# RWKV WKV on one core: k and v loads, stores and state rows on other DMA queues

## The chip, the core and the metric

The kernel runs on one NeuronCore of a Trainium2 chip. The metric is the device time of one execution in microseconds (us), as the median of several executions. Engines are named as in the profile: PE (matrix engine), DVE (vector engine), ACT (scalar engine), POOL (GpSimd) and SP (the engine that here only issues transfers). A transfer that POOL issues goes through the software queue q0, one that SP issues through the hardware queue q1; both feed the same 16 DMA engines.

## The reference

A running weighted mean over time, for each of 16 batches and 256 channels, over 2048 time steps:

```python
for b in range(batch):
    aa, bb, pp = 0, 0, -1e38          # per channel
    for t in range(seq_len):
        kk, vv = k[b, t, :], v[b, t, :]
        ww = u + kk
        qq = np.maximum(pp, ww)
        e1, e2 = np.exp(pp - qq), np.exp(ww - qq)
        output[b, t, :] = (e1 * aa + e2 * vv) / (e1 * bb + e2 + 1e-08)
        ww = pp - w + kk
        qq = np.maximum(ww, kk)
        e1, e2 = np.exp(ww - qq), np.exp(kk - qq)
        aa, bb, pp = e1 * aa + e2 * vv, e1 * bb + e2, qq
```

k, v and the output are float32, 16 x 2048 x 256: 33.5 MB each, so some 100 MB go between HBM and SBUF.

## The kernel before

Time lies on the partitions. The 2048 time steps are cut into a head of 32 and 16 steps of 126 (two halves of 63). A step's 16 batches are taken as four *pairs* of four batches each, so one pair is a tile of 126 time rows by 4 x 256 channels; loads take 128 rows where there are 128 left, and 126 in the last step. The head is cut into two special pairs that come third and fourth. `pairs` holds all 66 in the order in which they are worked.

For a pair n, `load(n)` (L108) brings k into `kr` and v into `vr`. `round_k` (L264, the copy on L271) rounds k on DVE, `logs` (L273) forms logarithms of weights as matmuls with constant matrices (PE, L287), `exps` (L294) exponentiates them into the tile `ez` (ACT, L303), `cast_v` (L307) casts v to `vb` on DVE (L311), and `times_v` (L314) multiplies the weights by v on DVE (L319). `sums` (L338) adds up a step's pairs on PE (L349). From these sums a small chain on PE, ACT and DVE (L356 to L461) computes the state that the step hands on. `carries` (L444) forms the state's weights as a tile `ab`, `turn_carries` (L453) turns it on PE, and `inject` (L458) copies it to `row` (L460) and sends it by DMA (L464) into two spare rows, `TC` and `TC + 1`, of the `ez` tiles of the step, so that the output matmuls take it in as if it were two more time rows. A step has two groups of `ez` tiles, j = 0 and 1, of two pairs each, and two rows, h = 0 and 1, for its halves.

Ten iterations after its load stage a pair is finished: `den` (L483, matmuls on L488) and `num` (L503, L509) on PE, `recip` (L492) as a logarithm and an exponential on ACT (L499, L500), `mult` (L513, L517) on DVE, and `store` (L519, L535) writes `rd` to the output.

The main loop (L580 to L621) interleaves all this by hand: iteration n loads pair n + 4, exponentiates pair n, sums pair n - 1, rounds and logs pair n + 1, and finishes pairs n - 10 and n - 11. The function `K` (L35) pins each engine's instructions in the order in which they are written, so every queue is in order, POOL's and SP's too.

What the change touches, by queue:

- SP carries, in order: k and v of the first two pairs, the ten small transfers of the head pairs (L122), k of pair 4, v of all pairs from 4 on, and, once per step, the four transfers of `inject` (L464). The very last store's second half goes on SP too.
- POOL carries the constants at the start, k from pair 5 on, and the stores, and computes nothing else in the steady part.
- `kpool` and `vpool` have four buffers, so the k load of pair n + 4 waits until `round_k(n)` has read its buffer, and the v load until `cast_v(n)` has. `rpool` has five, so `recip` of a pair waits until the store of the fifth pair before it has landed.
- A queue's transfers use eight completion semaphores in turn; a transfer waits until the eighth before it has landed.

Of the kernel before, what the change touches and what calls it, by code (L numbers as in the profile page):

```python
# [9 lines left out]
BF16 = mybir.dt.bfloat16  # L10
# [12 lines left out]
def kernel(  # L23
# [11 lines left out]
    def K(ins):  # L35

        block, e, new = nc.cur_bb.bb, ins.ins.engine, []
        for i in reversed(block.instructions):
            if i.engine == e:
                new.append(i)  # L40
                if i.name == pinned.get(e):
                    break
        for a, b in zip(new[1:], new):
            tc.add_manual_dep(b, a.name, mybir.DependencyInfo(
                mybir.DependencyClass.NoSync, mybir.DependencyReason.DATA), reason="order")
        pinned[e] = new[0].name
        return ins

    PE, DVE, SC, POOL, SP = nc.tensor, nc.vector, nc.scalar, nc.gpsimd, nc.sync
# [3 lines left out]
    TC = 2 * HS  # L53
# [6 lines left out]
    AHEAD = 4  # L60
# [14 lines left out]
    tiny = ctx.enter_context(tc.tile_pool(name="tiny", bufs=1))  # L75
# [18 lines left out]
    NP = len(pairs)  # L94
    kr_of, vr_of = {}, {}

    def is_head(n):
        return pairs[n][0] < 0

    def tiles_of(n):  # L100
        return 1 if pairs[n] == (-1, 1) else 2
# [6 lines left out]
    def load(n):  # L108
        kr = kpool.tile([128, 4, Dm], F32, tag="kr", name="kr")
        vr = vpool.tile([128, 4, Dm], F32, tag="vr", name="vr")  # L110
        kr_of[n], vr_of[n] = kr, vr
        c, p = pairs[n]
        if is_head(n):
            if p == 1:
                K(POOL.memset(kr[64:96, 0:2, :], 0.0))
                K(POOL.memset(vr[64:96, 0:2, :], 0.0))
            for t, x in ((kr, k), (vr, v)):
                for g in range(NG):
                    b = 6 * g + 4 * p
                    e = min(b + 2 * tiles_of(n), B)  # L120
                    if b < e:
                        K(SP.dma_start(out=t[g * GB:(g + 1) * GB, 0:e - b, :],  # L122
                                        in_=x[b:e, 0:T0, :].rearrange("n t d -> t n d")))
        else:
            t0 = T0 + c * TC
            r = min(128, T - t0)
            for t, x, eng in ((kr, k, SP if n <= AHEAD else POOL), (vr, v, SP)):
                K(eng.dma_start(  # L128
                    out=t[0:r, :, :], in_=x[4 * p:4 * p + 4, t0:t0 + r, :].rearrange("n t d -> t n d")))


# [9 lines left out]
    for n in range(2):  # L141
        load(n)
# [3 lines left out]
    def matrix(name, dt, width=128):  # L146
        return consts.tile([128, width], dt, tag=name, name=name)
# [53 lines left out]
    for n in range(2, AHEAD):  # L201
        load(n)
# [38 lines left out]
    Id, IdN, Lh, LhN, Lf, LfN = [matrix(x, BF16) for x in ("Id", "IdN", "Lh", "LhN", "Lf", "LfN")]  # L241
# [20 lines left out]
    EZ, X_of, KM = {}, {}, {}  # L262
# [67 lines left out]
    def group_of(c, j):  # L330
        return 2 * j if c == 0 else 1 + 2 * c + j
# [22 lines left out]
    st, AB = {}, {}  # L354
# [88 lines left out]

    def carries(c):  # L444

        ab = tiny.tile([128, 4, 2, 16], BF16, tag="ab16", name="ab16")
        f, f2 = st.pop((c, "phi")), tiny.tile([128, 2, 32], F32, tag="phi2", name="phi2")
        K(DVE.scalar_tensor_tensor(f2, st[c, "g"][:, 0:2], 1.0, f, ALU.max, ALU.min))
        K(DVE.tensor_mul(ab, AB[c].rearrange("p q h (j x) -> p (h j) q x", j=2),
                         f2.rearrange("p h (j x) -> p (h j) x", j=2).unsqueeze(2).broadcast_to([128, 4, 2, 16])))  # L450
        st[c, "ab"] = ab

    def turn_carries(c):  # L453
        d = bank("num", [128, D]) if wide else bank("den", [128, 2, D])[:, 0]
        K(PE.matmul(d[:, 0:128], st.pop((c, "ab")).rearrange("p m q x -> p (m q x)"), Id, start=True, stop=True))
        st[c, "d"] = d

    def inject(c):  # L458
        row = small.tile([128, 128], BF16, tag="row", name="row")
        K(DVE.tensor_copy(row, st.pop((c, "d"))[:, 0:128]))  # L460
        for j in range(2):  # L461
            for h in range(2):
                p = 64 * h + 32 * j
                K(SP.dma_start(out=EZ[group_of(c, j)][TC + h:TC + h + 1, 0:2, :, :].rearrange(  # L464
                                   "o q i (x c) -> o (q i x) c", c=128),
                               in_=row[p:p + 32, :]))

# [8 lines left out]
    def bank(tag, shape):  # L478
        pools = [psd, wide[0]] if wide and tag == "den" else [psn, wide[1], wide[1]] if wide else [psd if tag == "den" else psn]
        turn[tag] += 1  # L480
        return pools[turn[tag] % len(pools)].tile(shape, F32, tag=tag, name=tag)
# [37 lines left out]
    def store(n):  # L519
        o = RD.pop(n).rearrange("p i (n d) -> p (i n) d", n=2)  # L520
        if n % 2 == 1:
            EZ.pop(n // 2)
        if is_head(n):
            for g in range(NG):
                b = 6 * g + 4 * pairs[n][1]
                e = min(b + 2 * tiles_of(n), B)
                if b < e:
                    K(POOL.dma_start(out=out[b:e, 0:T0, :].rearrange("n t d -> t n d"),
                                     in_=o[g * GB:(g + 1) * GB, 0:e - b, :]))
        else:  # L530
            c, p = pairs[n]
            t0 = T0 + c * TC

            for a, b, eng in ((0, 2, POOL), (2, 4, SP)) if n == NP - 1 else ((0, 4, POOL),):
                K(eng.dma_start(out=out[4 * p + a:4 * p + b, t0:t0 + TC, :].rearrange("n t d -> t n d"),  # L535
                                in_=o[0:TC, a:b, :]))


    later = {}
    for c in range(-1, NST):  # L540
        s = last_of[c]
        work = [(s + 1, "sums", copy_sums), (s + 1, "last", turn_sums)]
        first, second = lambda c: state_step(c, 0), lambda c: state_step(c, 1)
        if c < 0:
            work += [(s + 2, "sums", split_sums), (s + 2, "act", state_logs),
                     (s + 3, "exp", state_weights), (s + 3, "pool", state_start)]
        else:
            work += [(s + 1, "last", split_sums), (s + 2, "first" if c else "exp", state_logs),
                     (s + 2, "sums", state_offsets), (s + 2, "sums", state_weights), (s + 2, "pool", first),
                     (s + 2, "act", inject_logs), (s + 3, "exp", inject_weights),  # L550
                     (s + 3, "pool", carries), (s + 3, "last", turn_carries), (s + 3, "last", inject)]
            if c + 1 < NST:
                work.append((s + 4 if c else s + 3, "pool", second))
            else:

                work = [(s + 1, "act", copy_sums), (s + 2, "sums", turn_sums), (s + 2, "sums", split_sums),
                        (s + 3, "first", state_logs), (s + 3, "sums", state_offsets), (s + 3, "act", state_weights),
                        (s + 3, "last", first), (s + 4, "act", inject_logs), (s + 4, "act", inject_weights),
                        (s + 4, "last", carries), (s + 5, "pool", turn_carries), (s + 5, "pool", inject)]
        for slot, where, f in work:  # L560
            later.setdefault((slot, where), []).append((f, c))
# [18 lines left out]
    for n in range(NP + LAG + 1):  # L580
        q, qp = out_at.get(n), out_at.get(n - 1)
# [3 lines left out]
        if n + AHEAD < NP:  # L585
            load(n + AHEAD)
# [26 lines left out]
        if out_qp:  # L613
            mult(qp, 1)
            store(qp)
# [37 lines left out]
```

## Time and profile before

| | |
|---|---|
| median of 10 executions | 332.19 us (330.02 to 337.02) |
| the profiled execution | 333.83 us, span of the profile 332.1 us |
| granted PE clock | 0.985 of full speed over the span |
| read from HBM, written to it | 68.10 MB, 33.55 MB: 306 GB/s over the span |
| stores L535 on POOL, issue to landing | 3.9 / 7.2 / 10.7 us (least, median, most) |
| loads L128, issue to landing | 4.1 / 7.9 / 12.8 us |
| state rows L464, issue to landing | 1.9 / 6.5 / 14.9 us |

The profile shows one execution. "Busy" is the time in which an engine runs instructions; the share of DMA is the time that packets took, summed over 16 engines, so it can pass 1.00 a little where packets of two queues overlap. A line such as `DVE vb L311 <- DMA vr<-in_v_dram: 2.8, 2, 2.7` reads: before instructions of line 311 that write `vb`, DVE stood idle for 2.8 us in total, 2 times, 2.7 at most, until a load of v had landed. The chain of waits is followed back from the last instruction: each piece released the next. An issue that SP's or POOL's order holds back shows as a wait of that queue, not of an engine.

### The profile page before, as it was taken

How to read it: one execution, taken by the hardware profiler on the slowest of the kernel's cores; microseconds unless marked ns; L12 is line 12 of the kernel's file. 1: busy time of each engine (PE TensorE's matmuls, PEld its weight loads, DVE VectorE, ACT ScalarE, POOL GpSimd, SP SyncE). 2: the span in 40 equal slices, each digit the busy share in tenths (PEclk: the TensorE clock that was granted, in tenths of full speed). 3: DMA queues.
4: the chain of work that ended last, by engine and by line, in shares of the span. 5: the costliest groups of instructions: out<-in, count | busy, mean ns of one | idle time of the engine just before them, and what ended most of it. 6: DMA issues, size and time to landing. Idle time of an engine off the chain costs nothing.

```text
span 332.1 us, 4061 instructions
## 1 busy us (share of the span) xinstructions
PE 283.4 (85%) x1183; PEld 136.4 (41%) x1200; DVE 284.3 (86%) x571; ACT 277.5 (84%) x310; POOL 114.5 (34%) x162
## 2 busy tenths in 40 slices
PE   0696989799999899999999999999899999689470
PEld 0333444344445444545444444445453545234130
DVE  2878798989898999999998989898999998777470
ACT  2647589699999999998999999999999998798690
POOL 6221224504343433425343424343333424022230
PEclk9999799999999999999999999999999999999996
DMA  7999959899999999999999999999999999745865
GB/s 251 257 333 326 289 177 321 265 311 330 330 370 337 372 335 377 346 371 316 376 343 359 370 361 365 337 371 337 370 335 370 315 288 304 246 131 161 242 182 167
DMA packets 59120, 102.47 MB, mean 309 GB/s; under 512 B 7610, under 2 KB 43162, under 8 KB 59098
## 3 DMA queue, kind: packets, MB, share of 16 engines
q0 software_dynamic: 19232, 65.27, 56.4%
q1 hardware_dynamic: 39858, 36.93, 36.8%
q8 instruction: 9, 0.15, 0.2%
q14 instruction: 13, 0.11, 0.1%
q10 hardware_dynamic: 8, 0.00, 0.0%
HBM read 68.10 MB, written 33.55 MB: 306 GB/s over the span
## 4 chain that ended last, share of the span: by engine, by line
PE 44%; DVE 26%; DMA 10%; ACT 10%; issue 6%; SPq 1%; POOL 0%; POOLq 0%; DVEq 0%; ACTq 0%
PE X L287 12%; PE num L509 11%; PE tot L349 11%; DMA vr<-in_v_dram 7%; DVE ez L319 6%; PE den L488 5%; DVE rd L517 5%; ACT ez L303 5%; DVE km L271 5%; PE den L365 4%; DVE vb L311 3%; DMA kr<-in_k_dram 2%; DVE tsum L372 2%; ACT rd L499 1%; DVE tb L423 1%
## 5 line engine op out<-in xcount | busy, mean ns | idle before, releaser
L535 POOL DMA_DIRECT2D out_dram<-rd x64 | 58.9, 920 | 171.9 <-ACT rd L500 81.1
L303 ACT ACTIVATE ez<-X 128x2048 bf16<-128x2048 f32 x58 | 107.8, 1859 | 4.6 <-PE X L287 4.6
L517 DVE TENSOR_TENSOR rd<-num,rd 126x512 f32<-126x512 f32 (+1 forms) x131 | 88.7, 684 | 8.7 <-issue 3.9
L319 DVE TENSOR_TENSOR ez<-ez,vb 126x2048 bf16<-126x2048 bf16 (+1 forms) x66 | 79.8, 1209 | 2.6 <-ACT ez L301 2.1
L499 ACT ACTIVATE rd<-den 126x1024 f32<-126x1024 f32 (+2 forms) x67 | 66.9, 999 | 9.0 <-PE den L488 8.4
L500 ACT ACTIVATE rd<-rd 126x1024 f32<-126x1024 f32 (+2 forms) x67 | 69.6, 1039 | 2.1
L287 PE MATMUL X<-km,NLE 128*128 128x512 f32 x128 | 52.8, 494 | 15.1 <-DVE km L271 14.0
L128 POOL DMA_DIRECT2D kr<-in_k_dram x61 | 48.0, 787 | 30.3 <-DVE km L271 11.6
L349 PE MATMUL tot<-ez,OHV 126*48 126x512 bf16 x128 | 50.1, 391 | 8.2 <-DVE ez L319 8.2
L509 PE MATMUL num<-ez,LfN 128*128 128x512 bf16 x128 | 49.0, 383 | 7.1 <-DVE rd L517 6.9
L349 PE MATMUL tot<-ez,OHE 128*48 128x512 bf16 x128 | 51.1, 399 | 0.0
L509 PE MATMUL num<-ez,IdN 126*128 126x512 bf16 (+1 forms) x131 | 49.8, 380 | 0.0
L271 DVE CAST km<-kr 126x1024 fp32r<-126x1024 f32 x64 | 44.7, 698 | 4.7 <-ACT km L205 4.7
L311 DVE CAST vb<-vr 126x1024 bf16<-126x1024 f32 (+1 forms) x66 | 45.2, 685 | 2.8 <-DMA vr<-in_v_dram 2.8
L287 PE MATMUL X<-km,NLZ 128*128 128x512 f32 x128 | 41.0, 403 | 0.0
L488 PE MATMUL den<-ez,Id 126*128 126x512 bf16 (+1 forms) x131 | 39.1, 378 | 0.9
L488 PE MATMUL den<-ez,Lf 128*128 128x512 bf16 x111 | 34.4, 378 | 5.0 <-DMA ez<-row 3.0
L287 PEld LDWEIGHTS X<-km,NLE 128*128 128x128 f32 x128 | 24.1, 196 | 27.7 <-DVE km L271 9.7
L287 PEld LDWEIGHTS X<-km,NLZ 128*128 128x128 f32 x128 | 24.8, 194 | 6.2 <-ACT ez L301 0.3
L349 PEld LDWEIGHTS <-OHE 128*48 128x48 bf16 x128 | 13.2, 103 | 33.3 <-issue 26.7
L509 PEld LDWEIGHTS <-LfN 128*128 128x128 bf16 x128 | 12.3, 96 | 31.8 <-issue 22.7
L509 PEld LDWEIGHTS <-IdN 126*128 126x128 bf16 (+1 forms) x131 | 12.7, 97 | 24.1 <-issue 22.1
(101 smaller groups left out, 204.5 us busy)
## 6 DMA issues: line engine op xcount, KB each, us to landing
out_dram<-rd POOLq DMA_DIRECT2D x63, 504.0 KB, 7.2
vr<-in_v_dram SPq DMA_DIRECT2D x60, 512.0 KB, 5.6
kr<-in_k_dram POOLq DMA_DIRECT2D x57, 512.0 KB, 7.9
vr<-in_v_dram SPq DMA_DIRECT2D x4, 504.0 KB
kr<-in_k_dram POOLq DMA_DIRECT2D x4, 504.0 KB, 11.7
kr<-in_k_dram SPq DMA_DIRECT2D x3, 512.0 KB, 5.9
ez<-row SPq DMA_DIRECT2D x64, 8.0 KB, 6.5
kr<-in_k_dram SPq DMA_DIRECT2D x3, 128.0 KB
```

Source lines behind the costliest of these rows:

```text
L271: K(DVE.tensor_copy(KM[n][0:r, 0:i, :], kr_of.pop(n)[0:r, 0:i, :]))
L287: K(PE.matmul(X[q][:, i, :], m[0:kr, :], km[0:kr, i, :], start=True, stop=True))
L303: K(SC.activation(ez_of(n)[:, 0:4:2], X[2][:, :, 0:i, :], ACT.Exp))
L311: K(DVE.tensor_copy(vb[0:r, 0:i, :], vr_of.pop(n)[0:r, 0:i, :]))
L319: K(DVE.tensor_mul(ez[0:r, 1:4:2], ez[0:r, 0:4:2], vb[0:r, 0:i, :].unsqueeze(1).broadcast_to([r, 2, i, D])))
L349: K(PE.matmul(TOT[c], m[0:r, :], ez_of(n)[0:r, q, i, :], start=n == first_of[c] and i == 0 and q == 0, stop=n == last_of[c] and i == tiles ...
L488: K(PE.matmul(d[:, i, :], m[0:r, :], ez_of(n)[0:r, q, i, :], start=q == 0, stop=q == 2, skip_group_check=True))
L499: K(SC.activation(rd[0:r, a, :], d[0:r, a, :], ACT.Ln, scale=RS))
L500: K(SC.activation(rd[0:r, a, :], rd[0:r, a, :], ACT.Exp, scale=-1.0))
L509: K(PE.matmul(d, m[0:r, :], ez_of(n)[0:r, q, i, :], start=q == 1, stop=q == 3, skip_group_check=True))
L517: K(DVE.tensor_mul(RD[n][0:r, i, :], NUM.pop((n, i))[0:r, :], RD[n][0:r, i, :]))
L535: K(eng.dma_start(out=out[4 * p + a:4 * p + b, t0:t0 + TC, :].rearrange("n t d -> t n d"), in_=o[0:TC, a:b, :]))
```

## The change

From the third pair on that is not a head pair (pair 4 in the order of work) k and v are both loaded by POOL. Every store is split by rows: 120 rows go on POOL and 6 on SP; for the last pair each of the two halves of the batches is split so. The state's tile `ab` is laid out with the group j outermost, so that both rows h of a group lie in 64 neighbouring partitions of `row`, and `inject` sends each group with one transfer into two partitions instead of two transfers into one partition each.

```diff
@@ load
-            for t, x, eng in ((kr, k, SP if n <= AHEAD else POOL), (vr, v, SP)):
-                K(eng.dma_start(
+            for t, x in ((kr, k), (vr, v)):
+                K((SP if n < 2 else POOL).dma_start(
                     out=t[0:r, :, :], in_=x[4 * p:4 * p + 4, t0:t0 + r, :].rearrange("n t d -> t n d")))
@@ carries
-        ab = tiny.tile([128, 4, 2, 16], BF16, tag="ab16", name="ab16")
+        ab = tiny.tile([128, 2, 2, 2, 16], BF16, tag="ab16", name="ab16")
...
-        K(DVE.tensor_mul(ab, AB[c].rearrange("p q h (j x) -> p (h j) q x", j=2),
-                         f2.rearrange("p h (j x) -> p (h j) x", j=2).unsqueeze(2).broadcast_to([128, 4, 2, 16])))
+        K(DVE.tensor_mul(ab.rearrange("p j h q x -> p h j q x"), AB[c].rearrange("p q h (j x) -> p h j q x", j=2),
+                         f2.rearrange("p h (j x) -> p h j x", j=2).unsqueeze(3).broadcast_to([128, 2, 2, 2, 16])))
@@ inject
         for j in range(2):
-            for h in range(2):
-                p = 64 * h + 32 * j
-                K(SP.dma_start(out=EZ[group_of(c, j)][TC + h:TC + h + 1, 0:2, :, :].rearrange(
-                                   "o q i (x c) -> o (q i x) c", c=128),
-                               in_=row[p:p + 32, :]))
+            K(SP.dma_start(out=EZ[group_of(c, j)][TC:TC + 2, 0:2, :, :].rearrange(
+                               "h q i (x c) -> h (q i x) c", c=128),
+                           in_=row[64 * j:64 * j + 64, :]))
@@ store
-            for a, b, eng in ((0, 2, POOL), (2, 4, SP)) if n == NP - 1 else ((0, 4, POOL),):
-                K(eng.dma_start(out=out[4 * p + a:4 * p + b, t0:t0 + TC, :].rearrange("n t d -> t n d"),
-                                in_=o[0:TC, a:b, :]))
+            for a, b in ((0, 2), (2, 4)) if n == NP - 1 else ((0, 4),):
+                for r0, r1, eng in ((0, 120, POOL), (120, TC, SP)):
+                    K(eng.dma_start(
+                        out=out[4 * p + a:4 * p + b, t0 + r0:t0 + r1, :].rearrange("n t d -> t n d"),
+                        in_=o[r0:r1, a:b, :]))
```

More of the change, by code (lines that the diff above doesn't have):

```diff
@@ L454, in turn_carries @@
         d = bank("num", [128, D]) if wide else bank("den", [128, 2, D])[:, 0]
-        K(PE.matmul(d[:, 0:128], st.pop((c, "ab")).rearrange("p m q x -> p (m q x)"), Id, start=True, stop=True))
+        K(PE.matmul(d[:, 0:128], st.pop((c, "ab")).rearrange("p j h q x -> p (j h q x)"), Id, start=True, stop=True))
         st[c, "d"] = d
```

## The prediction, made before the changed kernel ran

> **What bounds the kernel now.** I read the page first, then the time windows, the chain of waits, the list of waits, the DMA issues, and last the trace's single instructions and DMA packets.
>
> ```profile
> PE 283.4 (85%) x1183; PEld 136.4 (41%) x1200; DVE 284.3 (86%) x571; ACT 277.5 (84%) x310; POOL 114.5 (34%) x162
> ...
> q0 software_dynamic: 19232, 65.27, 56.4%
> q1 hardware_dynamic: 39858, 36.93, 36.8%
> ```
>
> ```profile
> 114.00:132.00 18.00, 17.02 (x75) 8.29 (x74) 17.04 (x34) 16.83 (x19) 7.10 (x9) 1.00 1.01 358
> ...
> 258.00:276.00 18.00, 17.03 (x74) 8.39 (x74) 17.05 (x33) 16.84 (x19) 7.05 (x9) 1.00 1.02 289
> 276.00:294.00 18.00, 14.86 (x64) 7.01 (x63) 14.48 (x27) 14.77 (x18) 2.95 (x3) 1.00 0.80 259
> ```
>
> The first rows are engines and queues (packets, MB, share). The window rows give us of PE, PEld, DVE, ACT and POOL, then clock, DMA share and GB/s. In the steady part PE, DVE and ACT are all busy 17 of 18 us: three engines that feed each other. The sixteen DMA engines are full too (share 1.01), POOL is 60% idle. The clock is 1.00, so no step has to be scaled for it. At 258 us the DMA share stays and the rate falls from 358 to 289 GB/s: this is where the last four pairs are loaded, with 126 rows instead of 128.
>
> ```profile
> 107.52 1.15 DVE ez L319
> 110.45 0.61 DVE rd L517
> ...
> 125.28 1.15 DVE ez L319
> ...
> 269.93 19.63 DMA vr<-in_v_dram
> 289.58 0.69 DVE vb L311
> ...
> 310.36 3.51 DMA ez<-row
> ```
>
> ```profile
> PEld L488 <- DMA ez<-row: 3.8, 2, 3.5
> ...
> PE den L488 <- DMA ez<-row: 3.0, 1, 3.0
> DVE vb L311 <- DMA vr<-in_v_dram: 2.8, 2, 2.7
> ```
>
> The chain repeats every 17.76 us (107.52 to 125.28), one step of four pairs, and in between it names engines only. DMA enters it at two late places: a v load that took 19.63 us, and the last state rows, for which PE stood 3.0 us. The list of waits (total, times, longest) agrees: in 332 us DVE waited 2.8 us for loads, nearly all of it (2.66) at 283.6. So bytes that move faster in the steady part are worth nothing; only these late places and the drain can pay.
>
> ```profile
> vr<-in_v_dram SPq DMA_DIRECT2D x60, 512.0 KB, 5.6
> kr<-in_k_dram POOLq DMA_DIRECT2D x57, 512.0 KB, 7.9
> ...
> ez<-row SPq DMA_DIRECT2D x64, 8.0 KB, 6.5
> ```
>
> ```profile
> L535 POOL DMA_DIRECT2D out_dram<-rd x64 | 58.9, 920 | 171.9 <-ACT rd L500 81.1 <-ACT y L435 61.2 <-DVE rd L517 16.6
> ...
> L128 POOL DMA_DIRECT2D kr<-in_k_dram x61 | 48.0, 787 | 30.3 <-DVE km L271 11.6 <-DMA kr<-in_k_dram 8.3 <-DVE kmh L271 3.6
> ```
>
> The sum is made against the profiled execution: 333.83 us, span 332.1 and 1.7 around it. It lies 1.64 us above the median of 332.19, so I carry the difference over, not the total.
>
> **Loads on POOL, steady part: 0.** 62 v loads (pairs 4 on) and one k load leave SP. POOL then issues 194 transfers, not 130: 62 v and 1 k at 0.787 us and one more half store, some 50 us more. In a step that is 4 x (0.92 + 0.787 + 0.787) = 10.0 of 17.76 us, so it fits. A v load now stands behind a store and a k load: 0.92 + 0.79 = 1.7 us later than on SP (before, v at 145.40 beside the store at 145.38). It waits for the cast of the pair four earlier (L311), and behind it in POOL's order stand the next store and k load; in DVE's order that cast follows directly on the product which that earlier store waits for, so nothing new is held. Landings by the order of q1's packets are 5.0 to 9.6 us, plus 1.7 is 11.3, against 17.76 until the cast that needs it. POOL's transfers take eight completion semaphores in turn, so each waits for the eighth before it. With three per pair that is at the closest a v load 4.1 + 3.5 + 1.7 = 9.3 us after a store, whose landing was 6.2 to 9.1; a wait of a us there would still be inside the slack of 6.4.
>
> Do sixteen engines carry it on one queue? A step moves 4 x 1.565 MB = 6.26 MB in 17.76 us, 353 GB/s. Where q1 was almost empty, q0 alone ran at 365 (61.75 to 64.25 us), 370 (204.5 to 205.75) and about 390 GB/s (150 to 151.5); with stores alone 230 to 260. By the queue rows a MB costs 56.4 / 65.27 = 0.86 points on q0 and 36.8 / 36.93 = 1.00 on q1 (packets of 4 KB for the most part against 1 KB), so 32.9 MB moved save some 4 points of DMA time: the headroom grows, and is worth 0 while compute sets the step.
>
> **Start: 0.** POOL is done with its constants at 6.4 us, and pair 4's buffers come free at 9.6 and 10.2; SP, busy with the head loads, issued these at 11.67 and 12.29. They go earlier, but DVE waits for no load there.
>
> **DVE beside more issues on POOL: +0.3 (0 to +4.8).** The trace's 64 wide casts of L311 last 682 ns where no POOL transfer is issued beside them (58) and 758 in the six others, at most 921. L319 shows no difference (1218 and 1217), nor L517 (684 and 683); L271, beside POOL in 52 of 64 cases, 702 against 682. At its place, 1.7 us after the cast, a v issue falls on L319 and costs nothing; I take some four more collisions. If every cast collided: 64 x 0.076 = 4.8.
>
> The Trainium skill speaks against this edit: "SBUF — State Buffer", section "Who interferes with whom", says that a cast in DVE's 2-port mode and GpSimd exclude each other for the whole instruction, and that such loads belong on SP or ACT. The rows above show a tenth of a us, not a block; were all 62 v issues to hold up a 0.68 us cast entirely, the rule would make it +42 us.
>
> **The late v load: -2.8 (-2.8 to 0).** By q1's packets the four v loads of 126 rows land 9.6 to 15.3 us after issue. Why: q1 has 39,858 packets, 35,548 of 1 KB and 2,048 of 256 B; 2,262 are left, which is 137 x 16 + 5 x 14. So 126-row transfers on SP run on 14 engines only, 36 packets each, against 32. On q0 14 half-size packets in the one 126-row half store (9 rows an engine, one odd) say 14 as well. Moved, a v load has nine 4 KB packets on each of 14 engines. k loads on POOL landed in the same stretch in 11.2 to 12.8 us. Pair 63's v load, issued at 263.8 + 1.7 = 265.5, lands at 278.3 at the latest by these, and is needed at 280.95: the wait goes. A semaphore wait of 2.6 us would eat this slack.
>
> **State rows in two transfers: +0.6 (-0.2 to +1.4).** The ab product keeps its element count (292 ns, x16) and is taken as unchanged. For the last step, SP issued the first group's rows at 309.81 and 310.36; they landed at 313.70 and 313.87, and PE started at 314.00. One issue instead of two: by the first one's landing the pair would be complete at 313.70, -0.2. But the split follows the rows (14 of 126 above), and the new destination has two: then the 32 packets of a row share one engine, as 32 packets of a full v load do, and those landed in at best 5.0 to 5.5 us (152.99 to 158.08): 309.81 + 5.5 = 315.3, +1.4. Lying between, the middle. In steady steps the rows of 149.63 are read at 163.18, 13.5 us later: hidden. In the first step, issue 44.59, use 48.84: middle of 47.5 and 49.9 is 48.7, just in time, 0 (0 to +1.1).
>
> Here too a page has a rule: "DMA: Bandwidth & Descriptors", section "Why a DMA increments its semaphore by 16 and not by 1", says a transfer uses the largest engine count up to 16 that divides the outer sizes of both sides. That is 14 for 126, as counted, and 2 for the merged rows; by it the term would be the upper end, +1.4.
>
> **Stores of 120 + 6 rows, and the drain: 0 (-0.8 to +0.75).** The 6 rows cost SP 65 short issues (0.35 us), 24 KB each. They wait for the same product as the large part; behind them on SP stand only the state rows. A rd buffer comes free when both parts have landed, some 16 us after issue at the earliest use. 120 rows give 8 packets an engine if it is 15 engines, 9 now: at 211 ns (4 KB packets after 292 us) -0.2 a store, four in the last 9 us, -0.8. Against it the last half pair goes from SP (324.22) to POOL behind the other half (323.88 + 0.75): up to +0.75.
>
> **Sum.** -2.8 + 0.6 + 0.3 + 0 = -1.9: 331.9 against 333.83, and 332.2 - 1.9 = 330.3 against the median, 0.6% faster.
>
> **Rivals.** A: the late wait stays or moves by a pair, because 126-row loads are slow on either queue (289 GB/s while the share was 1.02). For it: k loads landed in 11 to 13 us there too. Against: 14 packed engines of SP are relieved. Then 332.2 + 0.9 = 333.1.
>
> B, slower: collisions with DVE. Place L311 and L271; price 0.076 us a cast; it decides from about 40 collisions (3 us) on, when semaphore waits shift POOL's issues onto the casts. 332.2 + 4.8 with the late wait gone only in part (-1.4) and +0.6: 336.2. Against it: L319 shows nothing.
>
> C: one queue does not carry the stream. It decides below 353 GB/s: at 340 a step takes 18.4, +0.65 x 13 steps = +8.5, 340.7. For it the windows of stores alone (230 to 260); against it 365 to 390 with loads in them.
>
> **Numbers.** Forecast 0.52, own range 328.5 to 331.8; A 0.18; B 0.18; C 0.12. A measurement tells about 0.5% from no change, 1.7 us: the forecast puts 0.44 below 330.5 and 0.08 within; A is within; B and C are slower. Low end: -2.8 - 0.2 - 0.8 = 328.4, rounded to 328.0; high end 336.5, which takes in A and most of B; C is left out.
>
> **What would show it.** Right: DVE's list has no wait for vr above 0.5 us at the end; the period is 17.76; q0 near 97 MB, mean DMA share under 1.0; PE's last wait for ez<-row 3 to 4.5 us; L311 stays near 690 ns. Wrong: a longer period with casts over 720 ns (B), or with waits for vr and kr in mid-run (C); v waits near 283 (A); a wait for ez<-row in every step, which would mean that two-row transfers land in over 13 us.

## The result, and the profile after

The changed kernel takes 336.09 us (median of 15 executions, 334.22 to 337.78) where the kernel before, run beside it, takes 332.54 us (50 executions). The ratio is 1.0116 [1.0091, 1.0141]: 1.2% slower. Forecast was 330.3 us, 0.6% faster. Ratios here and below leave out executions more than 1.5% above the fastest of their kernel, so they can differ a little from the quotient of two medians, which are taken over all executions.

The profiled execution of after lasts 336.09 us with a span of 334.4 us, 2.3 us more than the profiled span of before; the medians differ by 3.55 us. So this pair of profiles shows about two thirds of the loss: the profiled execution of before lies 1.29 us above its kernel's median of 332.54, that of after on its own. The page of after, engines and queues:

```profile
PE 284.3 (85%) x1183; PEld 136.8 (41%) x1200; DVE 285.3 (85%) x571; ACT 277.8 (83%) x310; POOL 163.2 (49%) x226
...
q0 software_dynamic: 27424, 96.95, 86.9%
q1 hardware_dynamic: 7334, 5.25, 6.0%
```

Time windows of after, columns as in the prediction:

```profile
114.00:132.00 18.00, 17.03 (x75) 8.26 (x75) 17.05 (x33) 16.84 (x19) 9.76 (x12) 1.00 1.02 357
258.00:276.00 18.00, 16.96 (x73) 8.29 (x74) 17.01 (x34) 16.84 (x19) 9.67 (x12) 1.00 1.03 319
276.00:294.00 18.00, 14.90 (x59) 7.54 (x59) 13.66 (x26) 13.41 (x16) 4.37 (x5) 0.91 0.85 251
```

The move to one queue worked as forecast: 96.95 MB on q0, and PE, DVE and ACT are busy in the steady window to 0.01 us as before. From 276 us on, DVE works 0.8 us and ACT 1.4 us less than before in the same window, and the granted clock is 0.91. The list of waits of after (total, times, longest) and its chain (start, length):

```profile
PEld L486 <- DMA ez<-row: 3.6, 2, 2.6
DVE km L271 <- DMA kr<-in_k_dram: 3.4, 3, 2.3
...
PE den L486 <- DMA ez<-row: 2.7, 2, 2.1
...
POOL kr L128 <- DMA vr<-in_v_dram: 2.0, 3, 0.9
```

```profile
44.39 4.95 DMA ez<-row
...
311.41 3.26 DMA ez<-row
```

The wait for v (2.8 us in all) is gone, and 3.4 us of waiting for k stand in its place, at 279.2, 285.8 and 291.2 us. The last line shows POOL itself held until an earlier load of v had landed: the eight semaphores. The first step's rows, issued at 44.39, are a new piece of the chain: PE now waits for them at 49.4 us. Counted from the last turn of `ab`, the last rows are read 0.9 us sooner than before.

To set the kernels side by side I cut the span at starts of the product of L319 (for pairs 15, 61 and 65), at the last product of L515 (L517 before) and at the end, in us:

| stretch | before | after | after less before |
|---|---|---|---|
| start to pair 15 | 71.91 | 72.45 | +0.54 |
| pair 15 to 61 (steady) | 203.70 | 203.63 | -0.07 |
| pair 61 to 65 | 20.15 | 21.30 | +1.15 |
| pair 65 to the last product | 28.44 | 28.96 | +0.52 |
| drain | 7.93 | 8.05 | +0.12 |

### The profile page after: what moved, and what is told of

The parts are those of the page before. It is cut to its first block, busy times and chain, and to the rows that moved or that the text cites. A ratio compares the mean times of both kernels' runs of the same rounds, so it can differ in the third digit from the quotient of the medians.

```text
span 334.4 us, 4174 instructions
## 1 busy us (share of the span) xinstructions
PE 284.3 (85%) x1183; PEld 136.8 (41%) x1200; DVE 285.3 (85%) x571; ACT 277.8 (83%) x310; POOL 163.2 (49%) x226
## 3 DMA queue, kind: packets, MB, share of 16 engines
q0 software_dynamic: 27424, 96.95, 86.9%
## 4 chain that ended last, share of the span: by engine, by line
PE 42%; DVE 26%; DMA 13%; ACT 8%; issue 6%; POOL 1%; SPq 1%; POOLq 0%; DVEq 0%
PE num L507 11%; PE X L287 11%; PE tot L349 9%; DVE ez L319 6%; PE den L486 6%; DMA kr<-in_k_dram 5%; DMA vr<-in_v_dram 5%; DVE rd L515 5%; DVE km L271 5%; PE den L365 4%; ACT ez L303 4%; DVE vb L311 3%; DMA ez<-row 2%; DVE tsum L372 2%; ACT rd L497 1%
## 5 line engine op out<-in xcount | busy, mean ns | idle before, releaser
L515 DVE TENSOR_TENSOR rd<-num,rd 126x512 f32<-126x512 f32 (+1 forms) x131 | 89.0, 685 | 9.3 <-issue 4.0
L319 DVE TENSOR_TENSOR ez<-ez,vb 126x2048 bf16<-126x2048 bf16 (+1 forms) x66 | 79.8, 1210 | 1.5 <-ACT ez L301 1.0
L497 ACT ACTIVATE rd<-den 126x1024 f32<-126x1024 f32 (+2 forms) x67 | 66.9, 999 | 10.5 <-PE den L486 9.9
L128 POOL DMA_DIRECT2D vr<-in_v_dram x62 | 48.0, 774 | 19.3 <-DVE vb L311 11.1
L507 PE MATMUL num<-ez,LfN 128*128 128x512 bf16 x128 | 49.7, 388 | 8.7 <-DVE rd L515 8.4
L128 POOL DMA_DIRECT2D kr<-in_k_dram x62 | 49.3, 796 | 11.7 <-DVE km L271 6.0
L271 DVE CAST km<-kr 126x1024 fp32r<-126x1024 f32 x64 | 44.9, 701 | 8.3 <-ACT km L205 4.8
L507 PE MATMUL num<-ez,IdN 126*128 126x512 bf16 (+1 forms) x131 | 50.6, 386 | 0.0
L311 DVE CAST vb<-vr 126x1024 bf16<-126x1024 f32 (+1 forms) x66 | 45.1, 683 | 0.3 <-DMA vr<-in_v_dram 0.3
## 6 DMA issues: line engine op xcount, KB each, us to landing
kr<-in_k_dram POOLq DMA_DIRECT2D x4, 504.0 KB, 13.6
```

Source lines behind the costliest of these rows:

```text
L128: K((SP if n < 2 else POOL).dma_start(out=t[0:r, :, :], in_=x[4 * p:4 * p + 4, t0:t0 + r, :].rearrange("n t d -> t n d")))
L271: K(DVE.tensor_copy(KM[n][0:r, 0:i, :], kr_of.pop(n)[0:r, 0:i, :]))
L319: K(DVE.tensor_mul(ez[0:r, 1:4:2], ez[0:r, 0:4:2], vb[0:r, 0:i, :].unsqueeze(1).broadcast_to([r, 2, i, D])))
L497: K(SC.activation(rd[0:r, a, :], d[0:r, a, :], ACT.Ln, scale=RS))
L507: K(PE.matmul(d, m[0:r, :], ez_of(n)[0:r, q, i, :], start=q == 1, stop=q == 3, skip_group_check=True))
L515: K(DVE.tensor_mul(RD[n][0:r, i, :], NUM.pop((n, i))[0:r, :], RD[n][0:r, i, :]))
```

## Experiments: one part at a time

Ratios are to the kernel before, run beside each kernel, with 95% intervals. In each diff the left side is the whole change unless said otherwise.

**Loads alone** (before, with the hunk of `load` only), **stores alone** (the hunk of `store` only), **rows alone** (the hunks of `carries`, `turn_carries` and `inject` only).

```diff
-            for t, x, eng in ((kr, k, SP if n <= AHEAD else POOL), (vr, v, SP)):
-                K(eng.dma_start(
+            for t, x in ((kr, k), (vr, v)):
+                K((SP if n < 2 else POOL).dma_start(
```

> Before with the loads alone moved to POOL; stores and state rows as before. Theory 1 (the loss is made by the loads: last pairs wait for k, and the head pair waits at the start): about the changed kernel's ratio, 1.010 to 1.016; DVE waits for kr near 279 to 291 us, some 3.4 us in all, one wait of about 0.9 us near 20 us, landings of the last loads 13 to 15 us; middle period 17.76. Theory 2 (the loss is made by the stores or the state rows): ratio 0.995 to 1.000, since the late v wait of before (2.66 us) goes.

> Before with the stores alone split into 120 and 6 rows. Theory 1 (loads make the loss): ratio 0.998 to 1.003; the late v wait of 2 to 3 us stays, the drain after the last product is 8.6 us plus or minus 0.5. Theory 2 (stores make the loss): 1.006 or more, with a longer drain.

> Before with the state rows alone sent by two merged transfers. In the changed kernel the way from the turned state (L455) to the first output matmul that reads it took 4.07 us against 4.99 before, so theory 1 expects a gain of some 0.9 us: ratio 0.995 to 0.999. My prediction's step had +0.6 us: 1.002. Theory 2 (rows make the loss): over 1.005.

| run | median us | ratio |
|---|---|---|
| loads alone | 331.63 | 0.9942 [0.9902, 0.9981] |
| loads alone, run again later | 332.85 | 0.9972 [0.9937, 1.0006] |
| stores alone | 332.75 | 0.9973 [0.9927, 1.0019] |
| rows alone | 335.65 | 1.0055 [1.0005, 1.0106] |

Alone, loads and stores cost nothing and may win a little; merged rows lose. By the time, theory 1 falls: the loads alone do not make the loss. The trace of the first run of loads alone does show the late waits that theory 1 named, 3.5 us for k, but that execution lies 3.0 us above its median; the profile of the later run has 0.2 us of them. Added up the parts give -0.3% (0.0 with the later figure for the loads), the whole +1.2%: the loss is an interplay. The profile of rows alone shows something that no stretch of the whole kernel's profile does, a longer steady part (207.48 us for 203.70). Its waits and its chain:

```profile
PE den L486 <- DMA ez<-row: 5.0, 3, 2.2
DVE vb L311 <- DMA vr<-in_v_dram: 2.4, 2, 1.9
```

```profile
183.57 14.25 DMA ez<-row
...
219.73 15.80 DMA ez<-row
```

Two rows in mid-run took 14.25 and 15.80 us and stopped PE (0.59 us at 197.9, 2.16 us at 235.6), the second time with a half-clock window beside it. The ends of the queue's 256-byte packets suggest why. In a steady step of before, the last packets of the two groups of rows end about 4.4 and 5.9 us after the group's last issue; in after, 9.4 and 14.4 us, and there the second group's packets start only as the first's end. q1 of after has 4,608 packets of 1 KB, 2,048 of 256 B and 678 others, which is 14 x 16 + 32 x 2 + 65 x 6: a merged transfer runs on 2 engines. With all sixteen busy (share 1.02), the 32 packets of a row stand in line on one engine; before, 64 of the 137 transfers counted on 16 engines were such rows, with two packets on each engine. PE reads the rows some 13 us after issue, so in most steps it still comes out; in this execution it twice did not.

## Experiments: one part undone

**Rows as before** and **stores whole**, everything else changed:

> The changed kernel with the state rows sent as before (four transfers of one row); loads and stores as changed. Theory R (the merged rows cost most of the loss: each runs on two DMA engines, lands late and lets PE wait): ratio 0.990 to 0.998, like the loads alone (0.9942); no wait of PE for ez<-row outside the first and the last step. Theory S (the split stores together with the loads cost it): 1.006 to 1.014, like the whole change.

> The changed kernel with the stores whole on POOL as before; loads and merged rows as changed. Theory R: 1.005 to 1.014. Theory S: 0.995 to 1.003 (loads alone 0.9942 plus merged rows alone 1.0055).

Rows as before: 335.92 us, 1.0119 [1.0065, 1.0172]. Stores whole: 333.83 us, 1.0038 [0.9999, 1.0076]. So undoing the merged rows does not bring the time back (a second run, below, gives 1.0062), and the split of the stores, harmless alone, is part of the loss once the loads are on POOL. To place that, the **stores of the last twelve pairs whole**:

```diff
-                for r0, r1, eng in ((0, 120, POOL), (120, TC, SP)):
+                for r0, r1, eng in ((0, 120, POOL), (120, TC, SP)) if n < 54 else ((0, TC, SP if a else POOL),):
```

> The whole change, but the stores of the last twelve pairs are sent whole, as before (the last pair's second half on SP). Stores whole everywhere gave 1.0038, the whole change 1.0116. Theory L, the split costs only where the last loads and the last stores run together (after 260 us): the time falls to about that of stores whole, 333.5 to 334.5 us, ratio 1.002 to 1.006, and the wait for the late k loads falls from 3.4 us to under 2. Theory E, it costs something in the first two thirds, or nothing at all beyond the clock windows' chance: 335.5 to 336.7 us, ratio 1.009 to 1.014, with the late k wait still at 3 us or more.

336.32 us, 1.0113 [1.0073, 1.0153]: nothing won, so theory L falls by the time; what the split costs does not lie in the last pairs' stores. Its sign in the trace came all the same: in the profile, of the fastest of the twelve executions, the late waits for k are 1.5 us in place of 3.4. To see that the cost of the split was no chance of runs made apart, loads alone and rows as before ran once more, side by side on one chip:

> The loads alone on POOL, once more, on the same chip as a_norows_again. If the first figures hold, 0.990 to 0.998 and at least 0.8% below a_norows_again; if the two calls differed by chance, both lie at 0.999 to 1.006, within 0.5% of each other.

> Loads on POOL and split stores, rows as before, once more. If split stores cost over 1% beside these loads: 1.007 to 1.016, at least 0.8% above p_loads_again, and the profile shows a place where it goes (the last rows' issue on SP, late loads). If not: 0.999 to 1.006.

0.9972 [0.9937, 1.0006] against 1.0062 [1.0030, 1.0095]: 0.9% apart. The split does cost when the loads share its queue. The two profiled spans differ by 3.2 us, spread over all stretches (0.33 at the start, 0.38 in the steady part, 0.61, 0.78, and 1.15 in the drain). No one wait carries it, and the mechanism stays open.

**Wide loads.** The last step's loads fetch 128 rows for three of its four pairs; the two rows beyond belong to the next batch and are never used.

```diff
-            r = min(128, T - t0)
+            r = 128 if p < 3 else min(128, T - t0)
...
+                    bass.AP(tensor=x.tensor, offset=x.offset + (4 * p * T + t0) * Dm, ap=[[Dm, r], [T * Dm, 4], [1, Dm]])))
```

> The changed kernel, but in the last step three of the four pairs load 128 rows for k and for v; the two rows more are the next batch's first and nobody reads them. Same number of transfers, 1.6% more bytes in these six. Theory 1a (126-row loads are slow because of how 126 rows are split over the DMA engines): the rate in 262 to 287 us goes from about 300 to about 350 GB/s, landings of the last loads fall from 13-15 to 10-12 us, DVE's late waits for kr go from 3.4 us to under 1, ratio to before 1.000 to 1.006. Rival 1b (one queue is too slow in any case and the delay has piled up): landings stay over 13 us, the late waits stay over 2.5 us, ratio 1.010 or more.

332.73 us, 0.9992 [0.9954, 1.0029]: the whole loss is gone. The windows of this kernel:

```profile
258.00:276.00 18.00, 17.06 (x75) 8.30 (x74) 17.04 (x34) 16.83 (x19) 9.97 (x13) 1.00 1.02 354
276.00:294.00 18.00, 17.01 (x75) 8.30 (x74) 16.78 (x32) 16.69 (x19) 5.10 (x7) 1.00 0.75 239
```

At the same DMA share the rate from 258 to 276 us is 354 GB/s in place of 319, no wait for k is left, and pairs 61 to 65 take 17.60 us in place of 21.30. So the slow 126-row loads cause the late wait of this kernel. That they run on 14 engines is counted for SP's transfers of 126 rows and for one store on POOL; for loads on POOL the records do not tell. The same edit elsewhere, on the **kernel before** and on the **loads alone**, was to win as much there:

> The kernel before, with 128 rows in three pairs of the last step. Same cause: the v wait of 2.66 us near 283 goes, 20.15 to 17.6 us from pair 61 to 65, ratio 0.990 to 0.995. Rival: the wait stays (v is on SP, whose packets are of 1 KB), ratio 0.998 or more.

> Loads alone on POOL, and in the last step three of four pairs load 128 rows (two rows more that nobody reads). If 126 rows are the cause of the late waits in every variant, as the changed kernel's 21.30 to 17.60 us from pair 61 to 65 says: waits for kr of 3.5 us go, 20.65 to 17.6 us, ratio 0.983 to 0.990. Rival (the gain there was made by something only the changed kernel has): 0.992 or more.

It missed: 1.0007 [0.9974, 1.0039] and 1.0012 [0.9977, 1.0047]. Pairs 61 to 65 do shrink to 17.53 and 17.54 us. Both profiles have half-clock windows at 35 to 43 us and at 311 to 316 us, and drains of 9.13 and 8.75 us; that this is what gives the gain back on the median is not shown.

**v of pairs 4 to 15, and pair 4's k, on SP as before:**

```diff
-            for t, x in ((kr, k), (vr, v)):
-                K((SP if n < 2 else POOL).dma_start(
+            for t, x, eng in ((kr, k, SP if n <= AHEAD else POOL), (vr, v, SP if n < 16 else POOL)):
+                K(eng.dma_start(
```

> The whole change, but pair 4's k and the v loads of pairs 4 to 15 stay on SP as before. Theory start: the loads issued ahead of the first step's rows cost about 2 us (pair 15 starts at 72.5 us with the loads on POOL, 70.3 with v on SP, where no clock window falls). So pair 15 starts at 70.2 to 70.7 us without a clock window before it (up to 72 with one), no wait for the first rows near 49 us, and the time is 333.8 to 334.5 us, ratio 1.003 to 1.006. Rival: the 2 us only bring the late k loads' need forward and are given back there: the wait for k after 275 us grows from 3.4 to 5 us or more and the time stays at 335.5 to 336.5 us, ratio 1.009 to 1.013.

333.97 us, 1.0008 [0.9965, 1.0052]: theory start holds by the time, while the ratio lies below the expected 1.003 to 1.006. In its profile pair 15 starts at 70.79 us, the wait for the first rows is gone, and 2.9 us of late waits for k remain:

```profile
DVE km L271 <- DMA kr<-in_k_dram: 2.9, 3, 1.6
...
PE den L486 <- DMA ez<-row: 2.2, 1, 2.2
```

Over all twenty profiles of this study PE waits for the first step's rows in the ten with the early v loads on POOL (0.18 to 1.54 us), and in none of the ten with them on SP. The start sorts by two things. Without a half-clock window before 43 us pair 15 starts at 70.3 to 70.8 us with v on SP (four profiles) and at 72.5 with the loads on POOL (two). With one or two windows it is 71.9 to 72.6 (six) and 72.5 to 74.1 us (eight). The order at the start costs about 2 us, and the windows cost up to 2 more by chance.

**Nine matmuls that nothing reads**, while PE waits for the last rows:

```diff
+            if q == first_of[NST - 1]:
+                busy = pst.tile([48, D], F32, tag="tot", name="tot")
+                for i in range(9):
+                    K(PE.matmul(busy, IdN[0:TC, 0:48], ez_of(q)[0:TC, 3, 0, :], start=i == 0, stop=i == 8,
...
             den(q)
```

> The whole change with nine extra matmuls of 48 columns by 512 (1.95 us at 0.216 us each) on PE where it waits for the last rows; nothing reads them. Theory clock: the window of half clock follows PE's idle time there; with PE busy it does not come, the stretch from the first output matmul of the last step to the last product is 9.5 us in place of 10.9 in the profile, and the median falls by 0.5 to 1.4 us (334.7 to 335.6 us, ratio 1.007 to 1.010). Rival: the windows do not follow the idle time, or the late k wait's window matters alone: a window still falls behind the rows' wait, or the median stays at 335.8 us or more, ratio 1.0105 or more.

335.55 us, 1.0059 [1.0018, 1.0100]. One time window each of after and of this kernel, behind the wait for the last rows:

```profile
315.00:318.00 3.00, 2.83 (x8) 1.10 (x8) 0.69 (x1) 1.60 (x2) 0.00 (x0) 0.51 0.80 250
```

```profile
315.00:318.00 3.00, 2.79 (x13) 1.19 (x13) 0.94 (x2) 1.40 (x2) 0.54 (x1) 1.00 0.86 224
```

PE is busy in both, with 8 matmuls at clock 0.51 and 13 at 1.00. The stretch from pair 65 to the last product takes 27.68 us for 28.96. The gain of the median, 0.5%, has about the size of the trace's 1.3 us; the intervals overlap, so its size on the median is not shown.

**What these edits say together.** Three single edits, stores whole, wide loads, and v on SP at the start, each take 0.8 to 1.2% off a loss of 1.2%, so their shares cannot be added up. Nor does the late wait for k in a profile order the medians: 3.5 us of it stand beside 0.9942 (loads alone), 2.9 beside 1.0008 (v on SP at the start), and 0.2 beside 1.0119 (rows as before). The late wait is what the profiled execution of after lost most by; what the median's loss is made of stays open beyond these three edits.

## Experiments: a version that beats both

**Combined**: v on SP up to pair 15, then all loads on POOL, wide loads, stores whole, merged rows. Then the same with **four row transfers**, and with the **nine matmuls**.

> What the runs so far speak for: v of pairs 4 to 15 and pair 4's k on SP as before, k and v of all later pairs on POOL, stores whole on POOL, merged rows, and the last step's loads of the first three of its four pairs taken with 128 rows. If the start (2 us) and the late wait (2.6 us) are both won and nothing is given back: 329 to 331 us, ratio 0.990 to 0.995. If the tail gives it back, as with the wide loads on the kernel before (1.0007) and with the loads alone and wide (1.0012): 332.0 to 333.5 us, ratio 0.998 to 1.002, with a drain of 8.7 us or more or a clock window in the tail.

> c_best with the state rows sent by four transfers per step as before. If the later landing of merged rows costs nothing but slack, the time is c_best's plus the last step's 0 to 0.9 us: 331.4 to 332.6 us, ratio 0.995 to 0.999. If merged rows cause waits in the steady part in some executions, as in the profile of the rows alone, the time falls: 330.0 to 331.0 us, ratio 0.990 to 0.994.

> c_best with the nine unread matmuls while PE waits for the last rows. If the half-clock window there costs what the trace shows (10.9 against 9.5 us from the first output matmul of the last step to the last product) in most executions: no window behind the rows' wait and 330.0 to 330.9 us, ratio 0.990 to 0.9935. If the windows only come elsewhere, or cost little on the median: 331.2 us or more, ratio 0.994 to 0.998.

Last, four row transfers **again** beside the same kernel **without wide loads**, which differs from the kernel before in one expression:

```diff
-            for t, x, eng in ((kr, k, SP if n <= AHEAD else POOL), (vr, v, SP)):
+            for t, x, eng in ((kr, k, SP if n <= AHEAD else POOL), (vr, v, SP if n < 16 else POOL)):
```

> c_rows4 once more, beside c_narrow. If its figure holds: 0.985 to 0.992. If it was chance: 0.994 to 1.000.

> The kernel before with one line changed: v of pairs 16 and later is loaded by POOL; last step's loads with 126 rows, stores whole, four row transfers. If the 128 rows carry the gain of c_rows4: waits for k of 2.5 to 3.7 us after 275 us as in the loads alone, and 0.8 to 1.1% above c_rows4_again, ratio 0.996 to 1.001. If the order at the start does, by freeing SP's queue from v in the steady part: within 0.4% of c_rows4_again.

| run | median us | ratio |
|---|---|---|
| combined | 331.57 | 0.9952 [0.9920, 0.9985] |
| combined, nine matmuls | 331.34 | 0.9951 [0.9919, 0.9983] |
| combined, four row transfers | 329.56 | 0.9884 [0.9851, 0.9917] |
| the same again | 330.27 | 0.9893 [0.9846, 0.9940] |
| the same, 126-row loads | 331.90 | 0.9972 [0.9941, 1.0003] |

The combined kernel falls between the two cases of its expectation. The version with four row transfers is 1.1% faster than before both times that it ran, on 6 executions each. Merged rows cost it 0.7%, against the kernel with nine matmuls that ran beside it: more than slack, as the second case of that expectation had it. The wide loads carry 0.8%, though the one profile without them has no late wait (pairs 61 to 65 in 17.52 us): the ratio shows it, the trace does not. The nine matmuls bring nothing here on the median, although they remove the window and 1.4 us in the profile (27.58 for 28.97): the first case of that expectation missed. Windows of the fastest profile, the first of the two with four row transfers:

```profile
25.00:45.00 20.00, 15.34 (x68) 7.82 (x67) 17.69 (x48) 14.36 (x21) 3.59 (x5) 1.00 0.97 311
...
258.00:276.00 18.00, 17.03 (x75) 8.21 (x74) 17.05 (x33) 16.84 (x19) 9.98 (x12) 1.00 1.01 356
```

No window at the start (clock 1.00), none of the late rate loss (356 GB/s), pair 15 at 70.39 us, pairs 61 to 65 in 17.48. The repeated run's profile is 2.8 us longer, with windows at 34.8 to 41.6 and 311.3 to 314.7 us: that much is chance within one kernel.

## Why the prediction was wrong

**Loads on POOL, steady part: 0.** Right. 203.63 us for 203.70, and one queue carries 357 GB/s, so rival C fell.

**DVE beside POOL's issues: +0.3.** Right, or less. The groups of after:

```profile
L271 DVE CAST km<-kr 126x1024 fp32r<-126x1024 f32 x64 | 44.9, 701 | 8.3 <-ACT km L205 4.8
...
L311 DVE CAST vb<-vr 126x1024 bf16<-126x1024 f32 (+1 forms) x66 | 45.1, 683 | 0.3 <-DMA vr<-in_v_dram 0.3
```

683 ns for L311, with 10 of its casts beside an issue at 708 on average, 894 at most. Rival B fell: that its 336.2 us lies 0.1 from the measured time is luck. The Trainium skill's rule of whole-instruction exclusion ("SBUF — State Buffer", "Who interferes with whom"), which the prediction set aside by DVE's rows, does not show on the casts, but agrees with what POOL's side shows. In after, 117 of POOL's 194 loads and stores are issued with no cast of L271 or L311 beside them and take at most 0.83 us each. Of the 77 beside a cast 44 take longer, up to 1.43 us, where the cast took 0.68. The prediction priced DVE's side alone; what POOL's delay costs is not shown.

**The late v load: -2.8, "the wait goes".** This is the step that failed. v's wait went, but the cover that I gave it did not ask what now stands in front of k. Measured: +1.15 instead of -2.8, which is 3.95 of the 4.2 us between the sum of -1.9 and the profiled +2.3. DMA issues of after (KB each, median us to landing):

```profile
kr<-in_k_dram POOLq DMA_DIRECT2D x58, 512.0 KB, 8.9
vr<-in_v_dram POOLq DMA_DIRECT2D x58, 512.0 KB, 9.7
kr<-in_k_dram POOLq DMA_DIRECT2D x4, 504.0 KB, 13.6
vr<-in_v_dram POOLq DMA_DIRECT2D x4, 504.0 KB, 14.0
```

I took the 11.2 to 12.8 us in which 126-row k loads landed before, when v stood in another queue, and checked them against v's need alone. In one queue each k stands behind a v and a store: 13.6 us. And k is needed about 3 us sooner than v of the same pair, since the loop rounds a pair's k before it casts its v. The prediction also read the four 126-row v loads of before too early: by their completion semaphores they landed 15.6, 19.8, 19.6 and 14.1 us after issue, as its own chain line of 19.63 us says, and not the 9.6 to 15.3 us that the order of packets gave. The eight semaphores, which I weighed as "a wait of a us inside the slack of 6.4", held POOL's last loads by 0.5 to 1.1 us each, when the slack was gone. That is rival A's mechanism, "stays or moves by a pair", at a higher price. The late wait does not come in every execution: three profiles with 126-row loads on POOL (loads alone the second time, rows as before, the best version without wide loads) have at most 0.2 us of it. Their last two k loads land 10.5 to 12.5 us after issue, in after 14.0 and 15.1. All but one of the prediction's signs for being right came true (0.3 us of waits for v, the period, 96.95 MB on q0, a DMA share of 0.93, 683 ns for L311; only PE's last wait was shorter, 2.1 us), and the kernel was slower: no sign looked at k or at the start.

**Start: 0, and the first step's rows "just in time, 0".** Failed, by about 2 us. "They go earlier" was right, and their price was overlooked: pair 4's loads went out at 10.1 and 11.5 us, before the head's small transfers, whose issues on SP moved from 8.6 to 11.0 us to 10.3 to 14.0 us, and DVE waited 0.9 us for head k at 20.4. At 44 us, a v load that before was issued behind the rows on SP, at 47.18, goes out on POOL at 44.41, beside the first of them, and PE waits 0.59 us for rows. The two profiles hide most of it, since before happens to have a half-clock window there and after none; the run with v back on SP shows it.

**State rows: +0.6.** In this pair of profiles the last step gained 0.92 us (from the last turn of `ab` to the first output matmul of the step, 5.00 to 4.08). That this is the merging's gain is not shown: over the twenty profiles the same stretch takes 3.81 to 5.44 us with four transfers and 3.98 to 4.49 with two. The upper end of +1.4 did not come: its 5.5 us were a full load's packets under full queues, and in the drained tail the rows took 3.3. The Trainium skill's rule that I weighed, 2 engines for two rows ("DMA: Bandwidth & Descriptors", "Why a DMA increments its semaphore by 16 and not by 1"), agrees with the packet count, but not with the upper end that I put on it. "In steady steps: hidden" was wrong in part: in the profile of rows alone two groups took 14 to 16 us, against a use some 13.5 us after issue.

**Stores and drain: 0.** The drain is right (+0.12). The split's cost beside POOL loads, 0.9%, was not in the prediction, and its mechanism is not shown.

**The clock.** The prediction took it as 1.00 throughout. After has a window at 287.7 to 291.1 us behind the late k wait and one at 315.0 to 318.4 behind the last rows, where the profile of before has none; the second undoes the gain of the rows (10.93 us for 9.50 from the last step's first output matmul to the start of the last product).

## What to carry to other kernels

When a load is moved out of a waiting queue, work out the new landing of every transfer that then stands behind it, against its own time of need; a removed wait is won only if the next one in that queue has slack. Moving an issue earlier is not free when queues are full: ask which small, urgent transfer it now passes. Merging small transfers saves issues but can cut the engines they run on: with busy engines, count engines first, and keep urgent rows spread.

## What the runs showed of the hardware

- After 75 us the granted clock falls to 0.50 for windows of 3.41 us behind stretches in which PE was partly idle. With a grid of 3.41 us laid through the last such window of each of the twenty profiles, one followed wherever PE was busy at most 41% of a grid window, and none where it was busy 42% or more. The grid does not start with the kernel, so the same wait costs 1.4 us in one execution and nothing in the next. The Trainium skill describes the free-running window of 3413 ns ("TensorE: Matmul & The Clock Gate", "What's actually happening"), and asks for an idle window; here a window that was 41% busy was enough. Early in the kernel (26 to 60 us) windows that were 53 to 63% busy did either, and in eight profiles a half-clock window in which PE was busy throughout was followed by a second; these runs don't explain that.
- From 258 to 276 us the thirteen profiles with 126-row loads move 289 to 329 GB/s, and the seven with 128-row loads 346 to 359, all at a DMA share of 1.00 to 1.03.
- Merged rows, one transfer of 64 small packets on 2 engines: in after, from 62 to 275 us, their completion came 7.3 to 16.4 us after issue, in the last step 3.1 to 3.3.
- Issues of transfers by POOL last longer beside a cast on DVE: up to 1.43 us in after, and at most 0.83 with no cast beside them.
